# Making the low halves of a hybrid decoder's weights during the convolution and the up products instead of during the first gate

## The chip, the cores and the metric

One core of one Trainium2 chip runs the whole program in one launch. The metric is the device time in microseconds (us) of that one core. Three runs of the kernel before are known; their median is 2180.35 us.

## What is computed

The reference is a two-layer decoder trunk on 1024 tokens of width 1024, all in fp32. Layer 0 mixes tokens with a causal convolution module, layer 1 with sliding-window attention. Each layer then has a squared-ReLU MLP and a gated embedding:

```python
for i in range(DEPTH):                      # DEPTH = 2
    if i < N_A_LAYERS:
        y = conformer_conv(x, conv_w_in[i], ..., conv_w_out[i], conv_b_out[i])
    else:
        if i == N_A_LAYERS:
            kk, vv = shared_banded_kv(x, kv_w_k, kv_w_v, cos, sin)
        y = swa_sink_attention(x, attn_w_q[j], attn_sinks[j], attn_w_o[j], kk, vv, cos, sin)
    x = layer_norm(DEEPNORM_ALPHA * x + y, mix_ln_g[i], mix_ln_b[i])
    x = layer_norm(DEEPNORM_ALPHA * x + sq_relu_mlp(x, mlp_w_up[i], mlp_w_down[i]), ...)
    x = x + (p[i] @ ple_w_proj[i]) * jax.nn.sigmoid(x @ ple_w_gate[i])
```

## The kernel before

Every large product is made of three matmuls of rounded fp32 (`mm3`): high by high, high by low, low by high. So each weight tile is needed as a high half (the weight, cast to the rounded type) and a low half (the weight minus its high half). The plain way to make a unit of 128x1024 is `prep`: one load, one cast on ScalarE, one subtraction on VectorE. For some weights the low half is made ahead of time and parked in DRAM. `unit_ahead` does that for a unit: it loads two halves of 128x512, and for each of them `low_half` casts on ScalarE, subtracts on VectorE and stores 256 KB to a DRAM tile. Later `prep` with `low=` loads that tile instead of subtracting. `pair_ahead` does the same for a pair of blocks of the up weights, with four sums and differences (`form`) that the seven-product scheme of the MLP needs; it issues four loads, seven low halves and four form stores. `up_ahead` picks one of the two.

The program is first recorded as a list of operations. A planner (`Recorder.schedule`) then orders each engine's queue by list scheduling, with a price for each operation, a priority that is the place in the program, and a slot count for each tag of buffer (`SLOTS`). What it orders is issued in that order, and each engine and the one DMA queue (SP's) then run strictly in order, waiting on semaphores. Inside `later(by)` operations get a priority that is `by` places later. `nc.slack` adds that many ns to the time at which the planner takes an operation's inputs to be ready. For a DMA it counts on a landing 2800 ns after the issue at the earliest:

```python
dma = max(dma, t + 1400.0) + v.n * v.parts / 75.0
finish(o, max(dma, t + 2800.0))
```

The stages, in the order of time in the profile:

- 0 to about 260 us, `conv`: eight channel groups `c`. `conv_in` makes the gated input of a group and sends it through DRAM (`scr<-zz`, eight small stores for each half, then `B<-scr` loads of 256 KB). `taps` builds banded matrices (tag `E`) on VectorE, multiplies them with `B`, drains the result (ScalarE writes `g` in four pieces, VectorE adds the other half) and transposes `g` on TensorE with the planner's `SLACK` of 900 ns behind the drain. A loop over `n` interleaves the steps of the two, `taps` five steps behind.
- about 260 to 395 us: convolution norm, output projection with the first norm, embedding products, and low halves of layer 0's first up weights (`up_ahead(0, ...)`, tag `A`).
- about 395 to 710 us, the up products of `mlp(0)`: pairs `f` = 2, 4, ... 30, seven products each. The quarter `xh01`/`xl01` of the transposed activations isn't read any more once `token_forms` is done.
- about 710 to 1030 us: the down products and the second norm.
- about 1030 to 1165 us, `ple(0)`, the first gate: 16 output tiles. Behind each of them `ahead` makes one unit of low halves for the attention's weights (eight of `w_q`, eight of `w_o`, tag `X`), and behind four of them `up_ahead(1, ...)` makes those of the second MLP's first up blocks (blocks 0 and 1, pairs 2 and 4, tag `A`).
- from about 1165 us: keys and values, attention, and layer 1's MLP and gate.

Of the kernel before, what the change touches and what calls it, by code (L numbers as in the profile page):

```python
# [10 lines left out]
F32 = mybir.dt.float32  # L11
F32R = mybir.dt.float32r
# [3 lines left out]
P = 128  # L16
# [3 lines left out]
NT = T // P  # L20
HT = 512
# [26 lines left out]
MIX_GROUPS = (  # L48
    ((0, 1, 2, 3), (4, 5, 6, 7)), ((0, 1), (2, 3), (4, 5), (6, 7)),
)  # L50
# [6 lines left out]
LOW_BY = 400  # L57
# [5 lines left out]
DOWN = (0,), (1, 2), (3, 4), (5, 6), (7,)  # L63
LATER = ((18,), (18,))
AT = "A"
AHEAD = ((0,1), (2,)), {0: 0, 1: 1, 2: 2, 3: 4}
GRAIN = 64
SLACK = 900.0

# [37 lines left out]
class Buf:  # L107
    def __init__(self, tag, shape, dtype, space):
        self.tag, self.shape, self.dtype, self.space = tag, shape, dtype, space
        self.tile = None  # L110
        self.slot = None
        self.users = 0
        self.end = 0.0
        self.cells = {}
# [375 lines left out]
class Emit:  # L490
    def __init__(self, tc, d):
        self.tc = tc
        self.nc = Recorder()
        self.d = d
        self.hid_tags = ("A", "X")
        self.low = {}


    def const(self, name, shape, dt):
# [1 line left out]
        return self.nc.tile(name, shape, dt)  # L501

    def sb(self, tag, dt=F32, n=HT):
        return self.nc.tile(tag, (P, n), dt)

    def pair(self, tag, dt=F32):
# [223 lines left out]
    def conv(self):  # L730

        nc, d, ws = self.nc, self.d, self.ws
        cc = self.cc
# [152 lines left out]
        ins = (x for c in range(8) for x in conv_in(c))  # L886
        outs = (x for c in range(8) for x in taps(c))
        for n in range(32 + LAG):
            next(ins, None)
            if n >= LAG:  # L890
                next(outs, None)
# [47 lines left out]
    def mix_out(self, i, w, gb, tiles, lhs=None):  # L939

        nc, ws = self.nc, self.ws
        for cc in range(2):
            ws.add(*(w[4 * cc : 4 * cc + 4] if isinstance(w, list) else [w[cc, u] for u in range(4)]))
        for cc in range(2):
            us = ws.get(4)
            for g in MIX_GROUPS[cc]:
                pss = self.tok_group(g, us, lhs, last=g is MIX_GROUPS[cc][-1])
                if i == 0 and cc == 0:
                    for k in AHEAD[0][g is MIX_GROUPS[cc][-1]]:
                        self.up_ahead(0, k, AT)  # L950
                for ps, t in zip(pss, g):
                    xt = self.x[t][cc]
                    nc.vector.scalar_tensor_tensor(out=xt, in0=xt, scalar=ALPHA, in1=ps, op0=ALU.mult, op1=ALU.add)
                    if cc == 1:
                        self.layer_norm(t, gb, self.mid[i])
# [142 lines left out]
    def mlp(self, i):  # L1098
        nc, d, ws = self.nc, self.d, self.ws
        tags, xtags = (dict(zip((2, 1, 3, 4), "XAEB")), "EB") if i == 0 else (dict(zip((2, 1, 3, 4), "XEAB")), "AB")  # L1100
        first, last = list(range(HEAD[i])), list(range(NFF - TAIL, NFF))
        pairs = list(range(HEAD[i], NFF - TAIL, 2))
        for f in first:
            ws.add(*self.low.get((i, f), [d["w_up"][i, f]]))
        for f in pairs:
            ws.add(*(self.low.get((i, f)) or self.pair_units(i, f)))
        ws.add(*[d["w_up"][i, f] for f in last])

        us = ws.get(len(first[:4]))
        for h in range(2):  # L1110
            for f in first[:4]:
                self.store(i, f, (f % 2, h), self.up(f, h, us[f]))
        ws.done(len(us))

        def alone(f):
            c = {}
            for j in range(2):
                u = ws.get(1)[0]
                for h in range(2):
                    c[j, h] = self.up(f + j, h, u)  # L1120
                ws.done(1)
            self.keep(i, f, c)

        for f in first[4::2]:
            alone(f)

        T = self.token_forms(tags)
        plain = {
            (a, h): [self.xs(k + 4 * a, h * HT, HT) for k in range(4)]
            for a, h in ((0, 0), (1, 0), (1, 1))  # L1130
        }

        def prod(u, half, B, ps=None):
            wh, wl = u
            o = half * HT
            more = ps is not None
            ps = ps if more else self.ps()
            self.mm3(ps, [
                (wh[:, o + k * P : o + (k + 1) * P], wl[:, o + k * P : o + (k + 1) * P], *B[k]) for k in range(4)
            ], not more, True, more)  # L1140
            return ps

        def copy(ps, tag="t"):
            v = self.sb(tag)
            nc.scalar.copy(v, ps)
            return v

        def plus(a, ps):
            nc.vector.tensor_tensor(out=a, in0=a, in1=ps, op=ALU.add)
            return a  # L1150


        for f in pairs:
            w = ws.get(1)[0]
            p = prod(w, 0, plain[0, 0])
            c11 = copy(p)
            p2 = prod(w, 1, plain[1, 0])
            ws.done(1)
            w12 = ws.get(1)[0]
            prod(w12, 0, T[2], p)  # L1160
            c21 = copy(p)
            self.square(plus(c11, p2), "z")
            w34 = ws.get(1)[0]
            r = prod(w34, 0, T[3])
            prod(w12, 1, T[1], p)
            ws.done(1)
            c22 = copy(p, "bo")
            self.square(plus(c22, r), "z")
            w = ws.get(1)[0]
            prod(w34, 1, plain[1, 1], p)  # L1170
            c12 = self.square(p, "z")
            prod(w, 0, T[4], r)
            ws.done(2)
            self.square(plus(c21, r), "z")
            self.keep(i, f, {(0, 0): c11, (0, 1): c12, (1, 0): c21, (1, 1): c22})
            if f == LATER[i][-1]:
                self.mark = nc.ops[-1]
            if f in LATER[i]:
                self.keep_later(i, 2 * LATER[i].index(f))
        for f in last[::2]:  # L1180
            alone(f)

        self.x = []
        for t in range(NT):
            self.x.append(self.pair(xtags[t // 4]))
        self.begun = set()
        self.turn = 0
        for k in range(3):
            nc.move("tr", "ps")
        for n, cs in enumerate(DOWN):  # L1190
            self.down_seven(i, cs, n == 0, n == len(DOWN) - 1, list(range(NT)) if n == RES else [])
# [145 lines left out]
        t4 = tt(b21, b21, t2, sub)  # L1337
        product(a22, t4, [(1, 0)], two, own, end)

    def ahead(self, k):  # L1340

        w = ("w_q", "w_o", "w_up")[k // 8]
        with self.nc.later(LOW_BY):
            if k < 16:
                self.low.setdefault(w, []).append(self.unit_ahead(f"{w}{k % 8}", self.d[w][k % 8 // 4, k % 4], "X"))

    def up_ahead(self, i, k, tag):
        with self.nc.later(LOW_BY):
            if k < HEAD[i]:
# [4 lines left out]
    def ple(self, i):  # L1354
        nc, d, ws = self.nc, self.d, self.ws
        for cc in range(2):
            ws.add(*[d["w_gate"][i, cc, u] for u in range(4)])
        for cc in range(2):
            us = ws.get(4)
            cs = slice(cc * HT, (cc + 1) * HT)  # L1360
            for g in GATE_GROUPS[i][cc]:
                if i == 1 and cc == 1 and NT - 1 in g:
                    self.last_tile(us, cs)
                    break
                pss = self.tok_group(g, us)
                for ps, t in zip(pss, g):
                    if i == 0:
                        self.ahead(t + NT * cc)
                        if t % 4 == 3 and t // 4 + 2 * cc in AHEAD[1]:
                            self.up_ahead(1, AHEAD[1][t // 4 + 2 * cc], "A")  # L1370
                    xt = self.x[t][cc]
                    pr = self.sb("t")
                    nc.sync.dma_start(pr, self.proj[i][t][:, cs])
                    s = self.sb("t")
                    nc.scalar.activation(s, ps, AF.Sigmoid)
                    nc.vector.tensor_tensor(out=s, in0=s, in1=pr, op=ALU.mult)
                    nc.vector.tensor_tensor(out=xt, in0=xt, in1=s, op=ALU.add)
                    if i == 1:
                        nc.sync.dma_start(d["out"][t * P : (t + 1) * P, cs], xt)
                    else:  # L1380
                        h, f = t // PH, t % PH
                        nc.sync.dma_start(self.xsp[h][f : T // 2 : PH, cs], xt)
                        if cc == 1 and f == PH - 1:
                            self.phases_to_xT(h)
            ws.done(4)
# [336 lines left out]
```

## Time and profile before

| | |
|---|---|
| median of 3 runs | 2180.35 us (2180.21 to 2181.06) |
| the profiled execution | 2179.51 us, of it a span of 2177.7 us |
| TensorE (PE) | 2163.8 us busy, 10304 matmuls |
| weight loads of TensorE (PEld) | 1797.7 us busy |
| VectorE (DVE) | 1687.4 us busy |
| ScalarE (ACT) | 995.5 us busy |
| GpSimd (POOL) | 238.0 us busy |
| DMA | 361.90 MB, mean 166 GB/s |

PE is the matmul unit and PEld its weight loads, which overlap it. A row of instructions names engine, operation and tile (out<-in); the number behind "x" is a count. All engine operations carry the line L457, because the recorder issues them all from there; so groups are told apart by tile. A DMA issue is a row of SPq, SyncE's queue. In brackets stands how long an engine sat idle before an instruction, and what ended that. A matmul's end is modelled, so successive matmuls overlap in the listing: the distance between starts is the rate.

### The profile page before, as it was taken

To read this page: it belongs to the slowest core of one execution; us is meant where nothing else is said; L and a number is where in the kernel's file an instruction comes from. 1 tells how busy PE (TensorE), PEld (TensorE's weight loads), DVE (VectorE), ACT (ScalarE), POOL (GpSimd) and SP (SyncE) were. 2 spreads that over 40 slices of the span, in tenths; PEclk is the share of its full clock that TensorE was granted. 3 is DMA by queue.
4 is the path that set the end of the run, shared out by engine and by line. 5 is a ranking of instruction groups with operands and counts; after the bars stand their busy time and mean duration, and the time that the engine had idled before them with its cause. 6 is when DMAs were issued, how large, how long until landed. Compare 5 with 4: busy or idle time off the path is not lost. (4 is left out here: it accounts for less than half of the span.)

```text
span 2177.7 us, 29640 instructions
## 1 busy us (share of the span) xinstructions
PE 2163.8 (99%) x10304; PEld 1797.7 (83%) x10304; DVE 1687.4 (77%) x2826; ACT 995.5 (46%) x1834; POOL 238.0 (11%) x442
## 2 busy tenths in 40 slices
PE   9999999999999999999999999999999999999999
PEld 7888878888888888887888888888888888888887
DVE  7667788967776879879964888579777778888983
ACT  5233353644444533344546888445444453333441
POOL 0000042200000000001301444140000000000040
PEclk9999999999999999999999999999999999999999
DMA  7443644734565756552695022444446485565323
GB/s 234 117 116 85 189 161 163 262 127 155 174 213 170 257 163 219 182 183 83 218 343 203 21 78 79 149 146 167 162 162 213 162 290 171 168 222 171 101 68 102
DMA packets 169847, 361.90 MB, mean 166 GB/s; under 512 B 18656, under 2 KB 46688, under 8 KB 169696
## 3 DMA queue, kind: packets, MB, share of 16 engines
q1 hardware_dynamic: 169696, 360.00, 50.5%
q8 instruction: 81, 1.33, 0.3%
q14 instruction: 70, 0.57, 0.1%
HBM read 247.99 MB, written 111.94 MB: 165 GB/s over the span
## 5 line engine op out<-in xcount | busy, mean ns | idle before, releaser
L457 PE MATMUL ps<-xl,wh 128*128 128x512 f32 x616 | 240.5, 391 | 0.0
L457 PE MATMUL ps<-xh 128*128 128x512 f32 x618 | 240.4, 389 | 0.0
L457 PE MATMUL ps<-xl,xh 128*128 128x512 f32 x618 | 240.4, 389 | 0.0
L457 PE MATMUL ps<-xh,xl 128*128 128x512 f32 x618 | 240.4, 389 | 0.0
L457 PE MATMUL ps<-xh,wh 128*128 128x512 f32 x616 | 240.4, 393 | 0.0
L457 PE MATMUL ps<-xh,wl 128*128 128x512 f32 x616 | 240.3, 390 | 0.0
L457 ACT CAST wh<-raw 128x1024 fp32r<-128x1024 f32 (+2 forms) x144 | 133.0, 928 | 221.8 <-PE ps L457 141.3
L457 PE MATMUL ps<-wh,xh 128*128 128x512 f32 (+1 forms) x484 | 190.9, 394 | 0.8 <-ACT xh L457 0.7
L457 PE MATMUL ps<-wl,xh 128*128 128x512 f32 (+1 forms) x484 | 189.7, 392 | 0.0
L457 PE MATMUL ps<-wh,xl 128*128 128x512 f32 (+1 forms) x484 | 189.0, 391 | 0.0
L457 DVE TENSOR_TENSOR wl<-raw,wh 128x1024 fp32r<-128x1024 f32 (+1 forms) x112 | 117.1, 1046 | 56.2 <-ACT wh L457 55.9
L457 ACT CAST wh<-g 128x512 fp32r<-128x512 f32 x108 | 64.5, 621 | 169.5 <-PE ps L457 99.2
L457 PEld LDWEIGHTS ps<-xh,wh 128*128 128x128 f32 x616 | 116.0, 188 | 25.2 <-ACT xh L457 0.4
L457 PEld LDWEIGHTS ps<-xh,wl 128*128 128x128 f32 x616 | 116.0, 188 | 24.4
L457 PEld LDWEIGHTS ps<-xh,xl 128*128 128x128 f32 x618 | 116.0, 188 | 24.2
L457 PEld LDWEIGHTS ps<-xh 128*128 128x128 f32 x618 | 116.0, 188 | 24.0
L457 PEld LDWEIGHTS ps<-xl,xh 128*128 128x128 f32 x618 | 116.0, 188 | 24.0
L457 DVE TENSOR_TENSOR wl<-g,wh 128x512 fp32r<-128x512 f32 x108 | 72.0, 689 | 81.6 <-ACT wh L457 81.6
L457 PEld LDWEIGHTS ps<-xl,wh 128*128 128x128 f32 x616 | 116.0, 188 | 22.4 <-DVE xl L457 0.6
L457 ACT CAST xh<-wh 128x1024 fp32r<-128x1024 f32 x76 | 79.7, 1049 | 118.9 <-PE ps L457 114.1
L457 POOL TENSOR_SCALAR sm<-sm 128x1 f32<-128x1 f32 x40 | 13.5, 338 | 1029.9 <-DVE sm L457 1028.3
L457 DVE TENSOR_TENSOR E<-cst,g 128x1152 fp32r<-128x1152 f32 x64 | 86.1, 1353 | 43.3 <-PE ps L457 41.1
(331 smaller groups left out, 5272.6 us busy)
## 6 DMA issues: line engine op xcount, KB each, us to landing
wh<-hid SPq DMA_DIRECT2D x78, 512.0 KB, 4.3
raw<-in_w_up_dram SPq DMA_DIRECT2D x61, 512.0 KB, 3.7
wl<-in_w_down_dram SPq DMA_DIRECT2D x60, 512.0 KB, 4.6
hid<-zz SPq DMA_DIRECT2D x96, 256.0 KB, 2.9
hid<-t SPq DMA_DIRECT2D x70, 256.0 KB, 2.2
raw<-hid SPq DMA_DIRECT2D x30, 512.0 KB, 3.7
form<-A SPq DMA_DIRECT2D x33, 256.0 KB, 5.5
scr<-zz SPq DMA_DIRECT2D x128, 64.0 KB, 2.1
```

Of the source, the lines that this page charges most:

```text
L457: getattr(getattr(nc, o.eng), o.name)(*a, **k)
```

## The change

The sixteen units of `w_q` and `w_o` and the up blocks of layer 1 are no longer made behind the tiles of the first gate; `ahead` is gone. Instead:

- in the loop of `conv`, at steps `n` = 2 to 9, one unit of `w_q` each, and at steps 12, 14, 17 and 20 the up blocks 0 and 1 and the pairs 2 and 4 of layer 1. Their buffers are of tag `z` (four slots), which the convolution doesn't use otherwise.
- behind the pairs `f` = 6, 10, 14 and 18 of the up products of layer 0, two units of `w_o` each, in a new tag `Q`: the idle quarter `xh01` (for the loads) and `xl01` (for the low halves), four views each, handed out in turn.
- both are recorded with `later(LOW_BY)` (400 places) and with `nc.slack = WORK_SLACK`, 1000 ns.

```diff
-AHEAD = ((0,1), (2,)), {0: 0, 1: 1, 2: 2, 3: 4}
+AHEAD = (0, 1), (2,)
+WORK_SLACK = 1000.0
+CONV_WORK = {**{2 + k: (k,) for k in range(8)}, 12: (8,), 14: (9,), 17: (10,), 20: (12,)}
+UP_WORK = {6: (0, 1), 10: (2, 3), 14: (4, 5), 18: (6, 7)}
...
     def sb(self, tag, dt=F32, n=HT):
+        if tag == "Q":
+
+            k = dt == F32R
+            self.spot[k] += 1
+            return self.quiet[k][:, self.spot[k] % 4, :]
         return self.nc.tile(tag, (P, n), dt)
...
         for n in range(32 + LAG):
+            nc.slack = WORK_SLACK
+            for k in CONV_WORK.get(n, ()):
+                if k < 8:
+                    with nc.later(LOW_BY):
+                        self.low["w_q"].append(self.unit_ahead(f"w_q{k}", d["w_q"][k // 4, k % 4], "z"))
+                else:
+                    self.up_ahead(1, k - 8, "z")
+            nc.slack = 0.0
             next(ins, None)
...
+        if i == 0:
+            self.quiet = nc.tile("xh01", (P, 4, HT), F32), nc.tile("xl01", (P, 4, HT), F32R)
...
             self.keep(i, f, {(0, 0): c11, (0, 1): c12, (1, 0): c21, (1, 1): c22})
+            nc.slack = WORK_SLACK
+            for k in UP_WORK.get(f, ()) if i == 0 else ():
+                with nc.later(LOW_BY):
+                    self.low["w_o"].append(self.unit_ahead(f"w_o{k}", d["w_o"][k // 4, k % 4], "Q"))
+            nc.slack = 0.0
             if f == LATER[i][-1]:
                 self.mark = nc.ops[-1]
...
-    def ahead(self, k):
-
-        w = ("w_q", "w_o", "w_up")[k // 8]
-        with self.nc.later(LOW_BY):
-            if k < 16:
-                self.low.setdefault(w, []).append(self.unit_ahead(f"{w}{k % 8}", self.d[w][k % 8 // 4, k % 4], "X"))
...
                 for ps, t in zip(pss, g):
-                    if i == 0:
-                        self.ahead(t + NT * cc)
-                        if t % 4 == 3 and t // 4 + 2 * cc in AHEAD[1]:
-                            self.up_ahead(1, AHEAD[1][t // 4 + 2 * cc], "A")
                     xt = self.x[t][cc]
```

More of the change, by code (lines that the diff above doesn't have):

```diff
@@ L495, in __init__ @@
         self.hid_tags = ("A", "X")
-        self.low = {}
+        self.low = {"w_q": [], "w_o": []}
+        self.spot = [0, 0]
     def const(self, name, shape, dt):
@@ L948, in mix_out @@
                 if i == 0 and cc == 0:
-                    for k in AHEAD[0][g is MIX_GROUPS[cc][-1]]:
+                    for k in AHEAD[g is MIX_GROUPS[cc][-1]]:
                         self.up_ahead(0, k, AT)
```

## The prediction, made before the changed kernel ran

> **What bounds the kernel.** I read the page's busy times first, then the busy time of each engine by stage, then what TensorE waited for.
>
> ```profile
> span 2177.7 us, 29640 instructions
> PE 2163.8 (99%) x10304; PEld 1797.7 (83%) x10304; DVE 1687.4 (77%) x2826; ACT 995.5 (46%) x1834; POOL 238.0 (11%) x442
> ```
>
> ```profile
> core 0: us, PE busy (x) PEld busy (x) DVE busy (x) ACT busy (x) POOL busy (x), PEclk, DMA share, GB/s
> 0.00:40.00 40.00, 38.56 (x155) 30.93 (x156) 29.53 (x43) 23.41 (x38) 3.47 (x18) 1.00 0.82 252
> 40.00:250.00 210.00, 208.77 (x1179) 181.93 (x1179) 141.64 (x207) 66.99 (x163) 5.45 (x37) 1.00 0.44 115
> 395.00:710.00 315.00, 314.58 (x1395) 259.78 (x1393) 239.17 (x367) 142.35 (x235) 3.89 (x4) 1.00 0.54 184
> 1005.00:1050.00 45.00, 43.64 (x215) 35.54 (x214) 43.85 (x78) 24.07 (x37) 20.95 (x25) 1.00 0.29 86
> 1050.00:1165.00 115.00, 115.00 (x555) 95.44 (x554) 81.29 (x137) 57.85 (x116) 6.47 (x8) 1.00 0.84 293
> 1165.00:1400.00 235.00, 233.60 (x1312) 193.14 (x1311) 180.41 (x620) 177.92 (x522) 91.73 (x233) 1.00 0.29 94
> ```
>
> TensorE bounds every stage. The first gate (1050 to 1165 us), from which the work is taken, has 115.00 us of PE in 115.00, although DMA is at a share of 0.84 there. So the gate can't become shorter by being relieved. All of PE's waits together:
>
> ```profile
> PE ps L457 <- DVE t L457: 2.2, 3, 1.4
> PE ps L457 <- DMA B<-scr: 1.6, 3, 0.8
> PE ps L457 <- DVE g L457: 1.2, 2, 0.9
> PE ps L457 <- ACT t L457: 1.1, 3, 0.7
> PE tr L457 <- POOL X L457: 1.1, 2, 0.5
> PE tr L457 <- POOL E L457: 0.8, 1, 0.8
> PE ps L457 <- ACT xh L457: 0.7, 2, 0.3
> ```
>
> These seven groups are 8.7 us, and the longest single one (1.4) is the start of the program. The change leaves all 10304 matmuls as they are. Whatever it does must come out of these waits or add new ones.
>
> The instruments of the trace could hide some room. The Trainium skill (Perfetto Trace Analysis, Identifying the Most-Contended Engine) says that matmul busy time isn't a good measure of distance to the limit, and names the share of weight loads instead. By that measure, 83% here, there would be room; the trace agrees only that busy time can hide short pauses, and no row has a moved operation on TensorE.
>
> **What is moved.** In the gate stage it is these groups (duration is min/median/max in ns):
>
> ```profile
> L457 DVE TENSOR_TENSOR X<-X,X x32: 680/686/695, 1062.6 to 1187.5; 128x512 fp32r<-128x512 f32 x32
> L457 DVE TENSOR_TENSOR A<-A,A x26: 682/686/695, 1065.0 to 1133.8; 128x512 fp32r<-128x512 f32 x18, 128x512 f32<-128x512 f32 x8
> L457 ACT CAST X<-X x32: 612/622/667, 1020.0 to 1186.7; 128x512 fp32r<-128x512 f32 x32
> L457 ACT CAST A<-A x18: 602/618/666, 1017.5 to 1133.1; 128x512 fp32r<-128x512 f32 x18
> L457 SPq DMA_DIRECT2D w_q<-X x16: 319/356/1278, 1063.6 to 1122.2; - x16
> L457 SPq DMA_DIRECT2D X<-in_w_o_dram x16: 333/408/701, 1109.6 to 1174.9; - x16
> L457 SPq DMA_DIRECT2D form<-A x22: 319/320/761, 1081.7 to 1135.1; - x22
> ```
>
> To the convolution go 16 + 26 = 42 VectorE operations of 0.686 us (28.8 us), 16 + 18 = 34 ScalarE casts of 0.62 us (21.1 us), and DMAs of 256 KB each: 16 loads and 16 stores for `w_q`; for the up blocks 4 + 8 loads and 4 + 22 stores. That is 70 issues of some 0.36 us, 25 us of SP's queue, and 70 x 0.262 = 18.4 MB. To the up products go 16 VectorE operations (11.0 us), 16 casts (9.9 us), 32 DMAs (8.4 MB).
>
> **The gate and what follows: -0.7 us.** One PE wait touches the moved work. It lies in the keys and values, where the last `w_o` halves are still being made:
>
> ```profile
> 1172.71 0.60 PE L457 MATMUL tr<-ident,t 128*128 128x128 f32 x4
> 1173.83 0.66 PE L457 MATMUL ps<-ident,t 128*128 128x128 f32 x4 [0.52 <-DVE t L457]
> 1172.75 0.69 DVE L457 TENSOR_TENSOR X<-X,X 128x512 fp32r<-128x512 f32 x1
> 1172.08 0.63 ACT L457 CAST X<-X 128x512 fp32r<-128x512 f32 x1
> ```
>
> A subtraction for `w_o` runs from 1172.75 on VectorE, just ahead of the operation on `t` that PE waits for, and a cast sits on ScalarE before it. Without them `t` comes 0.69 us earlier, more than the 0.52. With the shorter pauses around it, hidden by the overlap, I put this at -0.7; between -1.4 (both moved operations were in its way) and 0 (another operation takes their place). The waits of the second norm (1005 to 1050 us: the 0.8 on POOL and one of 0.3 on `xh`) stay: the moved casts of that time, the first at 1017.5 and 1020.0, lie in gaps of ScalarE, while PE's waits end on POOL and on a norm's sum.
>
> **The start: +0.5 us.** The first `B` of the convolution is already late:
>
> ```profile
> 38.96 0.60 SPq L457 DMA_DIRECT2D B<-scr  x1
> 43.06 2.40 PE L457 MATMUL ps<-B,E 128*128 128x256 f32 x18 [0.36 <-DMA B<-scr]
> ```
>
> In the changed order two `w_q` loads stand in SP's queue before the last two input loads, and one store before this `B`; two casts stand on ScalarE between the last input casts. Three issues (3 x 0.36 = 1.1 us) and two casts (1.2 us) are not all in one chain; I take 1.4 us later. The order also puts 170 matmuls before the first `B` where 166 stood, which covers 4 x 0.226 = 0.9 us (the stage from 395 us has 1395 matmuls of this size in 315 us, 0.226 each). So +0.5; between 0 and +1.5 (2.3 less 0.9, rounded up). The input casts stay covered:
>
> ```profile
> 26.55 0.61 ACT L457 CAST xh<-X 128x512 fp32r<-128x512 f32 x1
> 29.62 0.39 PE L457 MATMUL ps<-xh,wh 128*128 128x512 f32 x1
> ```
>
> These are the last input's cast and, counted out in the order, the first matmul on it: 27.16 to 29.62, 2.5 us in hand, and the changed order puts that matmul seven places (1.6 us) later, which makes 4.1 against the 2.3.
>
> **The convolution after that: 0.** VectorE goes from 141.6 to about 170 of 210 us (81%), ScalarE from 67 to 88, DMA from 115 to about 200 GB/s; none of them is a bound. But everything that waits in a queue counts. Two chains are tight. First, `B` of each later group:
>
> ```profile
> 62.80 2.49 SPq L457 DMA_DIRECT2D B<-scr  x4
> 71.43 1.84 PE L457 MATMUL ps<-B,E 128*128 128x256 f32 x14
> B<-scr SPq DMA_DIRECT2D x24, 256.0 KB, 4.0
> X<-in_w_q_dram SPq DMA_DIRECT2D x12, 256.0 KB, 5.8
> B<-in_x_dram SPq DMA_DIRECT2D x3, 256.0 KB, 2.6
> ```
>
> Issue to use is 8.6 us, landing 4.0 (median, 50 to 250 us). At the gate's traffic a load took 5.8 us, which leaves 2.8; two more issues in front (0.7 us) leave 2.1. `B` stays covered. The Trainium skill (DMA: Bandwidth & Descriptors, Latency and other measured facts) gives an HBM access 0.2 us on average and 2 us at high load; an estimate by that page adds 1.8 us to the `scr` store and to the `B` load, 3.6 together, and the sum would still be 0, since 4.6 are in hand. The spread between 2.6 and 5.8 us in the rows above goes the way that page says.
>
> Second, the drain of the taps:
>
> ```profile
> 81.41 0.83 ACT L457 ACTIVATE g<-ps,cst 64x256 f32<-64x256 f32 x2 [0.19 <-PE ps L457]
> 83.70 0.69 DVE L457 TENSOR_TENSOR g<-g,ps 64x512 f32<-64x512 f32 x1
> 85.33 0.60 PE L457 MATMUL tr<-ident,g 128*128 128x128 f32 x4
> ```
>
> VectorE is done at 84.39, PE transposes at 85.33: 0.94 us in hand, which the planner's `SLACK` keeps in the changed order too. There, in most of the ten drains of the first 190 us, a cast of moved work stands on ScalarE in front of the drain's last piece. In about five of them its input comes straight from a load. The planner counts on 2.8 + 1.0 = 3.8 us for such a load. Loads took 2.6 us on quiet queues and 5.8 in the gate; the convolution lies between (4.0), so the cast is late by about 0.2 and the 0.94 hides it: 0, with an upper end of 5 x (5.8 - 3.8 - 0.94) = 5.3 us.
>
> **The up products: 0,** between 0 and +2. VectorE goes from 239 to 250 of 315 us. PE is busy there for 314.58 of 315 us. Views of a quarter that nobody reads cost no slot. The four early loads into that quarter for the down products are gated on the last operation recorded at `f` = 18, now a `w_o` store, and their place in SP's queue moves ahead, so they aren't late. **Everything behind:** the same instructions, with the order of the attention a little changed; its waits are 1.4 us of 235, half of it counted above, so between -0.8 and +1.5; I take 0.
>
> **The sum.** The profiled execution took 2179.51 us (span 2177.7 and 1.8 around it), 0.84 below the median of the three runs. -0.7 + 0.5 = -0.2 us on it gives 2179.3; against the median, 2180.2. No change can be told from less than 0.2%, 4.4 us.
>
> **Rivals.**
>
> 1. *Slower: late loads hold ScalarE in the drains.* If loads land as in the gate (5.8 us), five drains lose 1.06 each: +5.3, so 2180.2 + 5.3 = 2185.5 us. It decides from a mean landing of about 5.6 us on (five drains times 0.9). For it speaks that SP's queue is in order and carries 70 more issues, each of which can block behind a late store; against it, the 0.44 share of DMA now and the planner's added slack. Chance 0.12.
>
> 2. *Faster: the relief reaches more waits than the one.* Some casts leave ScalarE in the second norm, where PE waits 0.8 + 0.3 = 1.1 us, and the attention begins with its engines free (0.8). With 1.4 for the keys and values and a start that costs nothing that is -3.3, 2177.1 us, still within 0.2%. Beyond it only the hidden pauses could give more. Chance of over 0.2% faster 0.05.
>
> 3. *The start costs its full price* and the first groups of the convolution too, as their DMA share is 0.82 already: +1.5 and +2 in the up products, 2183.9 us with nothing won (2180.35 + 3.5). Chance 0.15, counted as no change.
>
> The change does what it says: the moved instructions do stand in the new places, and none is left in the gate.
>
> **How the numbers follow.** Likeliest (0.68): 2180.2 us. The low end takes the gate at -1.4 and the attention at -0.8, 2178.2. The high end reaches into the first rival, 2185.0. Faster 0.05, same 0.68 + 0.15 = 0.83, slower 0.12.
>
> **What would show it.** Right: 10304 matmuls and about 2164 us of PE; the gate at full PE with its DMA share well below 0.84; no wait on `t` near 1173 us; the first `B` waited for by about 0.9 us instead of 0.36; the convolution's end (about 250 us) later by less than 1 us. Wrong: PE rows in the convolution with waits on `g` or `B<-scr` before every group, a convolution that ends 3 us later or more, or a span shorter by over 4 us, which would mean that busy PE hid pauses that the moved work had caused.

## The result, and the profile after

The changed kernel is slower: 2188.43 us median of 6 runs (2187.36 to 2192.25), against 2180.28 (2179.80 to 2181.93, 6 runs) for the kernel before on the same chip. The ratio is 1.0038, 95% interval 1.0028 to 1.0048. That is outside the predicted range (2178.2 to 2185.0), on the side of the first rival.

The page of the profiled execution (2188.04 us) begins, with its busy line:

```profile
span 2186.3 us, 29570 instructions
PE 2164.2 (99%) x10304; PEld 1795.8 (82%) x10304; DVE 1686.3 (77%) x2826; ACT 999.0 (46%) x1834; POOL 238.8 (11%) x442
```

TensorE does the same 10304 matmuls in the same 2164 us of work. So the 8.6 us of added span are time in which it stood still, and the busy time by stage shows one place at once:

```profile
core 0: us, PE busy (x) PEld busy (x) DVE busy (x) ACT busy (x) POOL busy (x), PEclk, DMA share, GB/s
40.00:250.00 210.00, 205.26 (x1144) 177.54 (x1143) 160.82 (x240) 82.23 (x184) 5.45 (x37) 1.00 0.69 197
1050.00:1165.00 115.00, 113.88 (x554) 94.43 (x553) 55.83 (x96) 42.21 (x85) 10.98 (x11) 1.00 0.36 113
1165.00:1400.00 235.00, 232.85 (x1307) 191.21 (x1307) 175.21 (x611) 174.81 (x514) 89.48 (x233) 1.00 0.25 79
```

In 40 to 250 us PE is busy for 205.26 us instead of 208.77 and gets through 1144 matmuls instead of 1179. VectorE and ScalarE rose as forecast (160.82 and 82.23, where some 170 and 88 were expected), and neither is near a bound. The gate's DMA share did fall, from 0.84 to 0.36, but PE lost 1.12 us there, where it had been full. PE's waits in the whole span, the longest groups:

```profile
PE tr L460 <- DVE g L460: 3.3, 4, 1.5
PE ps L460 <- DMA B<-scr: 2.6, 3, 1.4
PE ps L460 <- ACT xh L460: 2.4, 2, 2.1
PE ps L460 <- DVE t L460: 1.6, 2, 1.4
PE ps L460 <- DVE xl L460: 1.3, 2, 1.1
...
PE ps L460 <- DVE sm L460: 0.6, 1, 0.6
```

The group on top is new: transposes of the convolution's drains that wait for `g`. The waits on `xl` and on `sm`, 0.2 us each before, have grown, in the gate and at the end of the attention.

Waits of 0.15 us and less aren't listed, so for the sums I use another reading. Both kernels run 10304 matmuls, so the start of the n-th can be set against the start of the n-th before; what the distance grows by between two marks is what that stretch lost (worked out from the traces). The marks are matmuls 200, 900, 4800, 5500, 5600 and 6800, which start at 48, 174, 1019, 1164, 1186 and 1396 us in the kernel before: the start, the convolution, everything up to the gate, the gate, keys and values, the attention with its output projection, the rest. One profile each, so tenths are not to be trusted, and from about the 5190th matmul on the order isn't the same in all (in the kernels with the convolution's part it differs in some earlier places too).

| kernel | start | conv. | to gate | gate | keys, values | attention | rest | sum |
|---|---|---|---|---|---|---|---|---|
| after | 1.9 | 4.1 | -0.2 | 1.2 | -1.6 | 2.8 | 0.3 | 8.5 |
| e1_conv_only | 1.0 | 4.4 | -1.6 | -0.1 | -1.6 | 3.2 | 0.1 | 5.5 |
| e2_up_only | 0.3 | 0.0 | 1.1 | 0.0 | -1.6 | 3.9 | 0.8 | 4.6 |
| e3_no_low | 0.3 | 0.0 | -1.0 | -0.1 | -1.5 | 3.2 | 1.2 | 2.1 |
| e4_attn_shift | -0.3 | 0.0 | 0.0 | 0.0 | 0.9 | -0.6 | 0.4 | 0.2 |
| f1_noload | 1.4 | 0.2 | -0.4 | 2.3 | -1.6 | 2.7 | 0.4 | 5.0 |
| f2_slack4 | 0.6 | 0.6 | -0.9 | 1.8 | -1.6 | 2.9 | 1.4 | 4.7 |
| f3_pool_cast | 1.5 | 0.0 | 0.4 | 1.9 | -1.6 | 3.1 | 1.7 | 6.9 |
| f4_attn_order | 1.9 | 3.8 | 1.7 | 2.0 | -1.6 | 3.4 | 0.3 | 11.6 |
| g1_up_q300 | -0.4 | 0.0 | 0.3 | 0.0 | -1.1 | 3.2 | 1.2 | 3.3 |
| g2_up_q800 | 2.7 | 0.0 | 0.6 | 0.0 | -1.0 | 3.0 | 0.5 | 5.8 |
| g3_up_q1500 | 0.7 | 0.0 | 2.1 | 0.3 | -1.1 | 3.6 | 0.1 | 5.7 |
| h1_up_s50 | -0.2 | 0.0 | 1.7 | 0.0 | -1.6 | 2.8 | 1.0 | 3.8 |
| h2_up_s400 | 0.7 | 0.0 | -0.7 | 0.0 | -1.6 | 3.9 | 0.1 | 2.4 |
| h3_before_s400 | 0.6 | 0.0 | -0.3 | 0.0 | 0.0 | 4.5 | 0.2 | 4.9 |
| h4_slack4_s50 | 1.3 | 0.6 | -0.1 | 1.8 | -1.6 | 2.2 | 0.4 | 4.7 |

The columns' own scatter can be read from kernels whose program is the one before in a stretch. The convolution of e2, e3, e4, g1 to g3 and h1 to h3 is unchanged: 0.0 nine times. Their start is unchanged as well, and there the column runs from -0.4 to 2.7. Six kernels with one and the same program up to 1147 us (e2, g1 to g3, h1, h2) have -0.7 to 2.1 under "to gate". And the seven kernels after, e1 to e3 and f1 to f3, in which every engine's queue has the same order from 1150 us on, have 2.7 to 3.9 under "attention". So the convolution's column is good to a tenth, the start's and the attention's are good to no better than a microsecond, and "to gate" to no better than two.

Four numbers of the table hold something else besides waits. In four of the profiles TensorE's granted clock is half of full speed for 3.41 us in the middle of the run, which takes up to 1.7 us: in the convolution of e1 (from 89.7 us), in the start of g2 (from 9.6 us), around the mark of 1019 us in g3 (from 1021.1 us) and in the attention of h3 (from 1369.6 us). In e1, 1.7 of the convolution's 4.4 us may be this, and 2.7 remain.

In the drains this is what a lost microsecond looks like. First ScalarE and VectorE, then SP's queue, then PE, of the changed kernel:

```profile
83.34 0.47 ACT L460 ACTIVATE g<-ps,cst 64x256 f32<-64x256 f32 x1 [0.19 <-PE ps L460]
87.22 0.62 ACT L460 CAST z<-z 128x512 fp32r<-128x512 f32 x1 [3.41 <-DMA z<-in_w_q_dram]
87.86 0.47 ACT L460 ACTIVATE g<-ps,cst 64x256 f32<-64x256 f32 x1
88.36 0.69 DVE L460 TENSOR_TENSOR g<-g,ps 64x512 f32<-64x512 f32 x1 [2.75 <-ACT g L460]
78.34 3.66 SPq L460 DMA_DIRECT2D scr<-zz  x8
82.10 0.38 SPq L460 DMA_DIRECT2D w_q<-z  x1
82.58 0.87 SPq L460 DMA_DIRECT2D z<-in_w_q_dram  x2
89.11 0.66 PE L460 MATMUL tr<-ident,g 128*128 128x128 f32 x4 [1.46 <-DVE g L460]
```

A drain has four pieces of `g` on ScalarE. Three are done by 83.81. Ahead of the fourth stands a cast of a `w_q` half, which waits 3.41 us for its load; the fourth piece, which had been ready, runs behind it at 87.86, VectorE adds at 88.36, and PE stands still for 1.46 us. The load had been issued at 82.58 at the earliest, because eight stores of `scr` had held the queue from 78.34 for 3.66 us and a store of `w_q` followed them. It landed by 87.22, 4.6 us after that. ScalarE's waits for the moved work from 40 to 215 us:

```profile
ACT z L460 <- DMA w_q<-z: 19.3, 9, 3.7
ACT z L460 <- DMA z<-in_w_up_dram: 9.8, 4, 3.5
ACT z L460 <- DMA z<-in_w_q_dram: 9.0, 3, 3.7
```

Sixteen waits, 38 us. Nine of them are not even for a load to land but for a store to free the buffer that the cast writes. These nine cost PE nothing that is listed: none of the nine casts stands directly in front of a piece of `g`. Five of the casts that wait for a load do, and four of these five drains have the four waits of PE on `g`. Two of those are nearly the whole of it: 1.46 us before 89.11 and 1.48 before 106.74.

The second of the two tells a slow landing from a late issue. Its load landed 3.1 us after its issue, sooner than the 3.8 that the planner counts on, and still the cast waited 3.65 us for it. It was issued at 101.65, behind eight stores of `scr` that held the queue from 94.84 for 5.41 us and a store of `w_q`, as in the first.

### The profile page after: what moved, and what is told of

Its sections match the earlier page's. It is cut to its first block, busy times and chain, and to the rows that moved or that the text cites. A ratio compares the mean times of both kernels' runs of the same rounds, so it can differ in the third digit from the quotient of the medians.

```text
span 2186.3 us, 29570 instructions
## 1 busy us (share of the span) xinstructions
PE 2164.2 (99%) x10304; PEld 1795.8 (82%) x10304; DVE 1686.3 (77%) x2826; ACT 999.0 (46%) x1834; POOL 238.8 (11%) x442
## 5 line engine op out<-in xcount | busy, mean ns | idle before, releaser
L460 PE MATMUL ps<-xh,wh 128*128 128x512 f32 x596 | 231.4, 392 | 2.1 <-ACT xh L460 2.1
L460 PE MATMUL ps<-xl,wh 128*128 128x512 f32 x596 | 233.0, 391 | 0.0
L460 PE MATMUL ps<-xh,wl 128*128 128x512 f32 x596 | 232.4, 390 | 0.0
L460 DVE TENSOR_TENSOR xl<-wh,xh 128x1024 fp32r<-128x1024 f32 x76 | 92.8, 1221 | 20.4 <-ACT xh L460 20.4
```

The source lines that it names most:

```text
L460: getattr(getattr(nc, o.eng), o.name)(*a, **k)
```

## The experiments

**First: which part of the change, and where.** Each half of the change by itself; the kernel before without the work; and the kernel before with another order of the attention.

e1: the convolution's part alone. `w_o` stays in the second half of the gate, tag `X`.

```diff
-UP_WORK = {6: (0, 1), 10: (2, 3), 14: (4, 5), 18: (6, 7)}
+UP_WORK = {}
...
                 for ps, t in zip(pss, g):
+                    if i == 0:
+                        self.ahead(t + NT * cc)
```

> The convolution's part of the change alone: w_q and the up blocks in the convolution, w_o back behind the tiles of the first gate. Theory A (loads that land late hold ScalarE's queue in the drains of the convolution, and the first B is later): the lag against before grows by 4 to 6 us between 40 and 180 us as in the changed kernel, 2184.5 to 2187 us in all. Rival B (the up products or their buffers cost the time): no lag before 400 us, 2180 to 2181 us. Rival C (the time is lost in the attention because its order is another): no lag before 1150 us, 2 to 3 us after.

Measured: 2184.71 us, ratio 1.0024 (1.0013 to 1.0035). The convolution lost 4.4 (up to 1.7 of it by the halved clock, behind a wait of 2.46 us on `g`), the attention 3.2.

e2: the part in the up products alone; `w_q` and the up blocks stay in the gate.

```diff
+UP_WORK = {6: (0, 1), 10: (2, 3), 14: (4, 5), 18: (6, 7)}
...
-            if k < 16:
+            if k < 8:
```

> The up products' part of the change alone: w_o there, w_q and the up blocks behind the first gate's tiles. Theory A: 2180 us within 1.5, no lag before 1100 us, and the wait of 0.5 us on t at the keys and values gone. Rival B (the up products): 3 us or more lost between 400 and 710 us. Rival C: whatever is lost stands between 1190 and 1400 us.

Measured: 2181.46 us, ratio 1.0009 (0.9999 to 1.0018). Up to the gate it lost 1.4 in all. The five kernels with the same program up to there lost -0.1 (g1) to 3.3 (g2), and those with the program of before -0.7 (e3) to 0.3 (h3), so one profile doesn't settle this sum.

e3: the kernel before without fifteen of the sixteen units of low halves; all sixteen read the one that is made, and nothing is made elsewhere.

```diff
-                self.low.setdefault(w, []).append(self.unit_ahead(f"{w}{k % 8}", self.d[w][k % 8 // 4, k % 4], "X"))
+                ap = self.d[w][k % 8 // 4, k % 4]
+                self.low.setdefault(w, []).append(lambda ap=ap: self.prep(ap, low=self.one))
```

> Leaves out 15 of the 16 units of w_q and w_o: one low half is made in the first gate, and all sixteen units read it. The up blocks stay in the gate. It bounds what taking this work out of the gate can bring. Theory A: the gate is bound by TensorE, so 0.7 to 1.4 us at most, 2179 to 2180 us, and 2 us either way from another order of the attention. Rival D (busy TensorE hides pauses that the work causes): 2175 us or less.

Measured: 2181.67 us, ratio 1.0007 (0.9998 to 1.0017). With the work gone altogether the kernel isn't faster: keys and values win 1.5, and the attention loses 3.2.

e4: the kernel before, with 300 ns of planner slack on the keys and values, which only gives the planner another order there and in the attention.

```diff
         kT = {(g, p): self.sb("B", F32R) for p in range(2) for g in range(4)}
+        nc.slack = 300.0
...
+        nc.slack = 0.0
         self.kT, self.k34 = kT, k34
```

> The kernel before with nothing moved; the planner alone is told 300 ns more for the inputs of the keys and values, which gives the attention another order of about the same size of difference as the change does. Rival C as luck of the order: the stretch from 1190 to 1400 us changes by 1 to 3 us, either way, and nothing before 1100 us. If the changed kernel's loss there comes from the moved work itself, this one stays within 0.5 us.

Measured: 2180.06 us, ratio 1.0002 (0.9993 to 1.0012); the attention's column is -0.6, with +0.9 in keys and values.

What follows: the convolution's loss comes with the convolution's part and with nothing else. The attention's loss comes with every kernel in which less stands in the gate's end, wherever the work went, even when it went nowhere.

**Second: what in the moved work costs the convolution its 4 us.** Loads, casts, subtractions and stores came together; three kernels change one each.

f1: the 28 loads are replaced by a fill on GpSimd; casts, subtractions and stores stay.

```diff
         r = self.sb(tag)
+        if tag == "z":
+            self.nc.gpsimd.memset(r, 0.5)
+            return r
```

> The changed kernel with the 28 loads of the work in the convolution left out: GpSimd fills each source buffer instead. Casts, subtractions and stores all stay. Theory A (ScalarE's queue is held by casts whose load hasn't landed): ScalarE's 38 us of waits for z loads go, TensorE's 3.3 us of waits on g in the drains go, and the lag between the 200th and the 900th matmul falls from 4.1 to under 1 us; 2184.5 us. Rival B (34 more casts and 42 more VectorE operations are simply too much beside the drains, or the stores hold SP's queue): 3 us or more of the lag stay, 2187 us or more.

f2: the planner counts on 4000 ns of slack instead of 1000 for the work in the convolution; all of it stays.

```diff
-            nc.slack = WORK_SLACK
+            nc.slack = 4000.0
```

> The changed kernel with the planner told 4000 ns instead of 1000 for the work in the convolution, so a cast is placed at the earliest 6.8 us behind its load. Theory A: the drains' waits shrink below 1 us in all, the lag from the 200th to the 900th matmul is 0 to 1.5 us, 2184.5 to 2186 us. If instead the load's issue is late by more than that (SP's queue held by stores ahead of it): the waits stay above 2 us.

f3: the 34 casts go to GpSimd; the loads stay as they are.

```diff
-        nc.scalar.copy(h, raw)
+        (nc.gpsimd.tensor_copy if tag == "z" else nc.scalar.copy)(h, raw)
```

> The changed kernel with the 34 casts of the convolution's work made by GpSimd instead of ScalarE; GpSimd is busy for 5 of 210 us there. Theory A in its narrow form (it is ScalarE's in-order queue that passes the delay on): no wait of ScalarE for z loads is left and the lag from the 200th to the 900th matmul falls below 2 us. If VectorE's queue passes the same delay on through its subtractions: waits of VectorE on GpSimd appear, and TensorE's waits on g stay above 2 us.

f4: the changed kernel with 1000 ns of slack on the keys and values (the diff of e4 with 1000.0), for a third order of the attention.

> The changed kernel with another order of the attention: the planner is told 1000 ns more for the inputs of the keys and values, nothing else. Theory C (the 2.8 us that the changed kernel loses between the 5600th and the 6800th matmul come from the order that the planner drew): that stretch changes by 1 us or more, most likely down, and the convolution keeps its 4 to 5 us; 2186 to 2188 us. If the loss there has to do with the work taken out of the gate itself, the stretch stays within 0.5 us of 2.8.

Measured: f1 2185.19 us, ratio 1.0022 (1.0013 to 1.0031); f2 2184.15, 1.0019 (1.0009 to 1.0028); f3 2185.94, 1.0028 (1.0018 to 1.0038); f4 2190.40, 1.0049 (1.0032 to 1.0066). PE's waits from 7 to 215 us, first in f1, then f2, then f3:

```profile
PE ps L460 <- DMA B<-scr: 0.9, 1, 0.9
```

```profile
PE ps L460 <- ACT xh L460: 0.8, 1, 0.8
PE ps L460 <- DMA B<-scr: 0.8, 1, 0.8
PE tr L460 <- DVE g L460: 0.4, 1, 0.4
```

```profile
PE ps L460 <- DMA B<-scr: 1.8, 1, 1.8
PE ps L460 <- ACT xh L460: 0.9, 1, 0.9
```

The wait on `g`, 3.3 us in the changed kernel, is gone without the loads, gone with the loads but the casts on another engine, and down to 0.4 when the planner allows the loads 4000 ns. So neither the load's traffic nor the cast's work costs it, but that the cast stands in front of a drain's piece in ScalarE's queue and waits for the load. In f2 ScalarE still waits 32.8 us for stores that free buffers (nine waits), more than in the changed kernel, and the convolution loses 0.6: how long it waits matters less than what stands behind. The wait didn't vanish from the chip in f3; it moved to where nobody needs the result soon. VectorE's waits there, 40 to 215 us:

```profile
DVE z L460 <- POOL z L460: 8.2, 11, 2.1
```

That VectorE waits 8.2 us for the casts of GpSimd costs PE nothing that the convolution's column shows (0.0). And f2 keeps every transfer: from 40 to 250 us its DMA share is 0.65 and its PE time 208.75 us, against 208.77 in the kernel before:

```profile
40.00:250.00 210.00, 208.75 (x1177) 181.41 (x1176) 156.81 (x235) 79.86 (x185) 5.47 (x37) 1.00 0.65 182
```

This part is settled. f4 says that a third order of the attention, too, loses there (3.4). Its time, 2190.40 us, is longer than the 2186 to 2188 expected.

**Third: is it the order of the attention, or the relief?** All relieved kernels but f4 had the same order of PE in the attention, so an unlucky order was still possible. Three more orders on e2, by planner slack on the passes of the attention (300, 800 and 1500 ns):

```diff
+        nc.slack = 300.0
         for gp in range(2):
             us = ws.get(4)
```

> As the run with only the up products' part, and 300 ns of planner slack on the operations of the attention's passes, which gives TensorE another order there (0.31 alike, by the share of instructions in common order) with the same instructions. Theory (the attention's loss belongs to the planner's order of that stretch, not to the relief of the gate): keys and values keep their -1.6 us; the stretch between matmuls 5600 and 6800 moves away from +3.9 by 1.5 us or more in at least one of these three runs, and the three differ from one another by over 1 us. Rival (the relief is given back: what came free in the keys and values is waited for again in the attention, whatever the order): +2.8 to +3.9 in all three, 2181.5 us each.

> The same with 800 ns, a third order. Theory: with operands planned 800 ns early fewer of them are late on the chip, so the attention's step comes out near 0 (-1 to +1.5) and the time about 2178.5 us, 1.5 below the kernel before. Rival (given back): +2.8 to +3.9, 2181.5 us.

> The same with 1500 ns, a fourth order. Theory: the attention's step differs from the others'; with so much slack the planner may run out of ready matmuls and leave PE idle in its own plan, so anything between -1 and +6 us, 2178 to 2184 us. Rival (given back): +2.8 to +3.9, 2181.5 us.

Measured: 2182.64 us, ratio 1.0010 (1.0001 to 1.0019); 2183.09, 1.0012 (1.0002 to 1.0021); 2184.13, 1.0016 (1.0006 to 1.0026). The attention lost 3.2, 3.0 and 3.6. My theory fell here: five orders with a relieved gate, and all lose about three. The rival's forecast for the attention (+2.8 to +3.9) came out, but its reason doesn't fit the sizes: keys and values won only 1.0 to 1.1 in these three, and the attention lost three times that. The times are 1.1 to 2.6 us above its 2181.5.

The traces show one place that the relieved kernels share. A group of scores goes through VectorE, ScalarE and GpSimd before PE can transpose it, and PE needs other work meanwhile. Near the end the kernel before has it. Here are the last six score matmuls of its last group but one, those of the last group, some of the projections that stand behind them, and at 1377.41 the transposes of the last group but one:

```profile
1368.94 0.96 PE L457 MATMUL ps<-B,g 128*128 128x256 f32 x6
...
1374.31 0.88 PE L457 MATMUL ps<-B,g 128*128 128x256 f32 x6
...
1375.95 0.40 PE L457 MATMUL tr<-wh,xl 128*128 128x512 f32 x1
1376.38 0.51 PE L457 MATMUL ps<-wh,X 128*128 128x512 f32 x1
...
1377.41 0.38 PE L457 MATMUL ps<-ident,z 128*128 128x128 f32 x2
```

The same in the changed kernel, from 1378.53 to the transposes at 1386.23:

```profile
1378.53 0.96 PE L460 MATMUL ps<-B,g 128*128 128x256 f32 x6
...
1382.12 0.50 PE L460 MATMUL ps<-B,g 128*128 128x256 f32 x2 [0.24 <-ACT g L460]
1382.46 1.02 PE L460 MATMUL ps<-A,bo 128*128 128x512 f32 x3
1383.58 0.98 PE L460 MATMUL ps<-B,g 128*128 128x256 f32 x6
1385.20 0.50 PE L460 MATMUL ps<-wh,X 128*128 128x512 f32 x1 [0.65 <-DVE sm L460]
...
1386.23 0.38 PE L460 MATMUL ps<-ident,z 128*128 128x128 f32 x2
```

It waits twice on the way, for 0.24 and 0.65 us, and loses more in pauses that aren't listed: the projections that filled such places are fewer. Counted in the order with the distances of undisturbed matmuls, the work between the last group of scores but one and its transposes is 7.2 us in the kernel before and 8.1 in e4; it is 4.8 in the changed kernel, e1, e2, e3 and all of f, and 5.5, 6.2 and 4.5 in g1 to g3. The real time in between was 7.8 (before), 8.2 (e4), 7.0 (changed) and 7.8, 8.0, 6.5 us (g1 to g3). So some 2 us are short there whenever the gate is relieved. Four runs on this cover:

h1: e2, with the scores of the last three tiles recorded 50 places earlier, which puts 7.4 us there. h2: 400 places earlier, which leaves the last four groups 3.3, 4.1, 6.0 and 6.2 us. h3: the same 400 in the kernel before, without any relief. h4: f2 with h1's edit.

```diff
-                    p = self.scores(n, 2 * gp + gl, qf[gl])
+                    with nc.later(-50 if gp and n > 4 else 0):
+                        p = self.scores(n, 2 * gp + gl, qf[gl])
```

> As the run with only the up products' part, but the scores of the last three tiles of the second pass are recorded 50 places earlier. Up to there the order of TensorE is the same; behind it, the matmul work that stands between the second-to-last group of scores and its own transposes rises from 4.8 to 7.4 us (33 score groups' distances counted in the order, with the trace's durations), for a chain that took 7.0 us. Theory (cover: the relieved planner runs the query projections ahead, and the attention's last groups lack them): the attention's step falls from +3.9 by about 2, to +1.5 to +2.3; the wait on the score maximum near the end goes; 2179.7 us. Rival (the relief is given back whatever stands there): +3 or more, 2181.5 us.

> The same with 400 places earlier, by which the last four groups of scores have only 3.3, 4.1, 6.0 and 6.2 us of matmul work before their transposes (8.1, 8.5, 4.8 and 6.7 without it). Theory (cover): 3.7 + 2.9 + 1.0 + 0.8 us short of 7.0, some of it shared by neighbours: the attention's step rises to +5 to +9, 2183 to 2187 us, with PE waits on the score maximum or its followers there. Rival: +3 to +4, 2181.5 us.

> The kernel before, nothing moved and nothing relieved, with the same 400 places: the last three groups of scores have 3.1, 5.8 and 5.6 us of matmul work before their transposes instead of 8.3, 7.2 and 7.8. Theory (cover): 3.9 + 1.2 + 1.4 us short, so +3 to +6 in the attention alone, 2183 to 2186 us, no change elsewhere. Rival (the loss comes with the relief of the gate, and needs it): 0, within 1 us of the kernel before.

> The whole change with 4000 ns of planner slack in the convolution's work and the scores 50 places earlier as above: both repairs together. Theory: the convolution's loss stays at about +0.6 and the attention's falls by 2, so 2 us less than with the slack alone, a ratio of about 1.001, 2182.5 us; what remains is the start (0.6 to 2) and the gate (+1.8). Rival: no less than with the slack alone, ratio 1.0019.

Measured: h1 2181.60 us, ratio 1.0002 (0.9993 to 1.0012); h2 2184.64, 1.0016 (1.0006 to 1.0025); h3 2184.73, 1.0017 (1.0008 to 1.0026); h4 2182.73, 1.0007 (0.9998 to 1.0016). PE's waits from 1320 to 1400 us, in h1 and then in h3:

```profile
PE ps L459 <- DVE A L459: 0.5, 2, 0.3
```

```profile
PE tr L457 <- ACT z L457: 1.5, 1, 1.5
PE ps L457 <- DVE A L457: 1.0, 1, 1.0
PE ps L457 <- DVE t L457: 0.2, 1, 0.2
```

h3's sum came out as expected: with nothing relieved, 3.0, 5.8 and 5.5 us of work before the transposes instead of 8.2, 7.2 and 7.8 cost the attention 4.5 us. But waiting is only a part of it. PE stands still for 2.7 of the 6.6 us up to 1369.60, and behind that its granted clock is 0.50:

```profile
1363.00:1369.60 6.60, 3.89 (x23) 2.85 (x22) 6.20 (x22) 5.47 (x16) 2.34 (x8) 1.00 0.03 14
1369.70:1373.00 3.30, 3.30 (x12) 2.54 (x11) 1.00 (x3) 0.77 (x2) 2.07 (x6) 0.50 0.00 0
```

3.41 us at half the clock are another 1.7 us. So cover at the attention's end is worth microseconds, in waits and once more in clock. Nine of h3's ten runs have a granted clock below 1.000 (to three places, over the whole run), and none of the 31 of the kernel before that ran with it.

In h1 the waits on `sm` and on ScalarE are gone, but the step fell from 3.9 to 2.8 only, 1.1 where about 2 was expected; in h4 from 2.9 to 2.2. Kernels with the same queues differ there by as much (2.7 to 3.9). By the whole times, too, each is a little nearer to the kernel before than the run that it changes (1.0002 after 1.0009, 1.0007 after 1.0019), with intervals that overlap, and h1's 2181.60 us is the rival's forecast. So the cover at the end may be about 1 of the 3 us; that it is isn't shown.

In h2's profile the thinner cover moved the waits (1.7 us of them on `z` from GpSimd) and added little to them: 3.9, not the 5 to 9 expected. But that profile is the fastest of h2's ten runs (2181.88 us), one of two at a granted clock of 1.000. The other eight show 0.998 or 0.999 and have a median of 2184.7 us, inside the 2183 to 2187 expected. What h2 usually costs can't be read from its profile.

So the attention's loss stays open for the most part. Some 0.6 us of it is how the cut falls: if the distance of each matmul to the next is reckoned against the usual one of its kind and its neighbours', the changed kernel wins 1.0 in keys and values and loses 2.2 in the attention. The rest is spread over small pauses that no row names. Nor did a run show why a relieved gate leaves less at the end. The order fits a planner that ran ahead: of the 128x512 matmuls with weights (`wh`, `wl`) behind its first score matmul, the changed kernel has 356 done by its 200th, the kernel before 332. But g2 has 331 and still loses 3.0, so this is an argument, not a finding.

No version beat the kernel before. Of those that do the whole change, h4, with both repairs, is the only one that can't be told from it.

## Why the prediction was wrong

**The bound, and the change itself: right.** 10304 matmuls, 2164.2 us of PE, a gate with a DMA share of 0.36, the moved operations off the gate.

**Gate and what follows, -0.7: right in sign and place, too small.** No wait on `t` is listed between 1160 and 1195 us any more. Keys and values won 1.6 by the marks (the range's end was -1.4), 1.0 with the cut allowed for.

**The gate itself, put at full PE: wrong, +1.2.** The kernels that leave nothing of the moved work in the gate lose 1.2 to 2.3 there; those that leave a part lose at most 0.3. In all six of the former VectorE waits 1.3 to 1.8 us for the same load, and PE then 1.1 to 1.6 us. VectorE, PE and SP's queue in the changed kernel:

```profile
1132.76 0.69 DVE L460 TENSOR_TENSOR t<-t,t 128x512 f32<-128x512 f32 x1 [1.31 <-DMA t<-proj]
1133.37 0.68 DVE L460 TENSOR_TENSOR xl<-ps,xh 128x512 fp32r<-128x512 f32 x1
1134.11 0.55 PE L460 MATMUL ps<-ident,B 128*128 128x128 f32 x3 [1.12 <-DVE xl L460]
1128.30 0.42 SPq L460 DMA_DIRECT2D t<-proj  x1
```

With the subtractions gone, VectorE reaches the product with `proj` 1.31 us before its load is there, and the operation on `xl` that PE needs stands behind it. In the kernel before the same queue was full of the moved operations, and the product ran without a wait; there the operations on `xl` stood ahead of it (1127.34 and 1128.54):

```profile
1129.13 0.69 DVE L457 TENSOR_TENSOR A<-A,A 128x512 fp32r<-128x512 f32 x1
1129.73 0.70 DVE L457 TENSOR_TENSOR t<-t,t 128x512 f32<-128x512 f32 x1
```

The planner's order of this queue changed together with the relief, and no run separates the two; that the moved operations had been padding is argued, not shown. The prediction had said that this stage can't become shorter by being relieved. It hadn't asked whether it can become longer.

**The start, +0.5: not decided, a little too small.** The first `B` was waited for as foreseen, and longer:

```profile
45.91 1.34 PE L460 MATMUL ps<-B,E 128*128 128x256 f32 x9 [1.44 <-DMA B<-scr]
```

1.44 us instead of the 0.9 expected. Another 2.1 us were lost on `xh` up to 8.5 us; but e2, whose start is the one before, waited 1.1 there and g2 1.7. The changed kernel's +1.9 is above the range of 0 to +1.5, but an unchanged start has -0.4 to 0.7 by itself, and 2.7 in g2 with its halved clock. Over the seven kernels with work in the convolution the column is 0.6 to 1.9, and 1.4 on average.

**The convolution after that, 0: the step that failed.** It measured +4.1. The prediction had named the chain (the cast in front of the drain's last piece), counted five drains, and given an upper end of 5.3. It then priced only the landing, at 4.0 us against the planner's 3.8, and let 0.94 us cover the difference. The landings were indeed near that (40 to 215 us):

```profile
z<-in_w_q_dram SPq DMA_DIRECT2D x14, 256.0 KB, 4.5
z<-in_w_up_dram SPq DMA_DIRECT2D x12, 256.0 KB, 3.6
B<-scr SPq DMA_DIRECT2D x24, 256.0 KB, 4.8
```

What was late is the issue: in the two drains that cost 1.46 and 1.48 us the load stands in SP's queue behind eight stores of `scr` and a store of `w_q`, and one of the two landed within 3.1 us. The first rival had the right place and nearly the price, and named the queue with 70 more issues as what speaks for it; its condition, landings from 5.6 us on, wasn't met and wasn't needed. `B` of the later groups stayed covered, as forecast: its median landing rose from 4.0 to 4.8 us (50 to 250 us). The estimate by the Trainium skill (DMA: Bandwidth & Descriptors, Latency and other measured facts) had put 1.8 us on that load at high traffic; here, with 197 GB/s instead of 115, it was 0.8.

**The up products, 0: right.** Between the 2044th and the 3438th matmul (395 to 708 us in the kernel before) the changed kernel lost 0.1 us, and no kernel but h4 (0.5) is further than 0.1 from the kernel before there. From 174 to 1019 us it lost -0.2.

**Everything behind, taken as 0 (-0.8 to +1.5): wrong too.** It measured +2.8 in the attention and +0.3 in the rest. The prediction had weighed PE's idle time of that stage (1.4 us of 235) and taken it to change little when the order changes. h3 shows that an order alone can cost 4.5 us there, 1.7 of it at half the clock. Why the relieved kernels lose there is open.

The sum by the marks: 1.9 + 4.1 - 0.2 + 1.2 - 1.6 + 2.8 + 0.3 = 8.5 us, the span's 2186.3 less 2177.7 but for rounding. The convolution is about half of it. Its 4.1 us alone would have ended near 2184.3 us, inside the range; the gate, the attention and the start took it out.

## What to carry to other kernels

When work with a load in front goes into an engine's in-order queue, price the whole way to that load, its issue behind the stores of its queue, and not the landing alone; then look at what stands behind the waiting instruction (here the last piece of a drain, up to 1.48 us of TensorE at a time). Leave such work on an engine that nobody waits for, or give the planner the real lateness: f3 and f2 did the same work in the same place for 0.0 and 0.6 us instead of 4.1 there, though both kernels stay slower than the one before (1.0028 and 1.0019). And taking work out of a stage whose bound it isn't can cost something: with the gate relieved, VectorE reached a load before it had landed (1.2 us), which may be the missing padding or the new order, and even the kernel without most of the work (e3) wasn't faster. Last, differences of 2 us can be the clock: look at the granted clock behind each long wait before a loss is put down to waiting alone.

## What the runs showed of the hardware

The same first 48 us of program took between 0.4 us less and 2.7 us more than in the profile before in nine kernels that don't change it, while the next 126 us agreed within 0.05 us in all nine. The loads that the program starts with land at times of their own: the fourth, issued at 2.1 us in each, landed at 5.0 us in e2 and at 8.1 us in g2. What depends on them can't be settled with one profile to a microsecond.

A cast of 128x512 took 961 ns on GpSimd, against some 620 on ScalarE, and the 31 of them from 40 to 215 us in f3 cost TensorE nothing that the convolution's column shows (0.0):

```profile
L460 POOL CAST z<-z 128x512 fp32r<-128x512 f32 x31 | 29.8, 961 | 82.8 <-DMA form<-z 24.9 <-DMA w_q<-z 15.9 <-DVE z L460 13.4
```

TensorE's granted clock fell to half for 3.41 us in the middle of four of the seventeen profiles. Each time that began 0.3 to 0.8 us after the end of a wait of TensorE: of 2.46 us in e1, 1.65 in g2, 1.99 in g3, and 1.50 in h3 with one of 1.04 just before. In e1 128x512 matmuls started 0.43 us apart meanwhile, instead of 0.23. Waits of 2.08 us in the changed kernel (at 8.5 us) and of 1.96 in f4 (at 1025 us) were followed by no such drop, so what decides it isn't shown.
